# Weight products in runs of eight k, one block of compression products, a 128-row compressed branch, and two more banks for the first output projection

## The chip, the cores and the metric

The kernel runs on one core of a Trainium2 chip. The metric is the device time of one execution in microseconds (us), as the median of several runs. The trace comes from one profiled execution. Engines: PE is TensorE (matrix products; PEld its weight loads), DVE is VectorE, ACT is ScalarE, POOL is GpSimd, SP is the queue that starts the DMA transfers.

## The reference, cut to what matters

A decoder of two layers over 256 tokens of width 1024, all in float32. Layer 0: one input projection feeds forgetting attention (8 heads) and retention (8 heads); their concatenated outputs are gated with SiLU and go through an output projection. Layer 1 is sparse attention with 16 query heads in 4 key groups and three branches: compressed, selected and window, whose outputs are added with gates.

```
def odd_layer(x, norm_g, w_in, b_gate, pe_k, pe_v, wk1, wk2, wv1, wv2, w_out):
    h = rms_norm(x, norm_g)
    u = h @ w_in                       # q, kc, vc, ks, vs, kw, vw, gate, z
    ...
    o = nsa_attention(...)
    return x + (o * jax.nn.silu(z)) @ w_out

def compress_blocks(a, idx, pe, w1, w2):
    ab = a[:, idx] + pe[None, None, :, None, :]       # 15 blocks of 32 tokens
    ab = ab.transpose(0, 1, 3, 2, 4).reshape(B, nc, NSA_KV_GROUPS, l * HEAD_DIM)
    return jax.nn.silu(ab @ w1) @ w2                  # w1: 2048 x 256, w2: 256 x 64

    # inside nsa_attention, per block of queries
    p_cmp = masked_softmax(s_cmp, ...)                # over 15 compressed keys
    o_cmp = jnp.einsum('bghqc,bcgd->bqghd', p_cmp, v_cmp)
    return g[..., 0:1] * o_cmp + g[..., 1:2] * o_slc + g[..., 2:3] * o_win
```

## The kernel before, in words

**Weight products and the feed.** Activations lie transposed: features on the partitions, 256 tokens in the columns. The weights come in 38 chunks of up to 280 columns by 1024 rows. A chunk is loaded by SP into `st`, and split in four quarters into a high half `wh` (fp32r, ScalarE, L95) and a low half `wl` (bf16, VectorE, L102). The activation is held in three forms: high `h`, low `l` (both fp32r) and `b` (bf16). One output tile of 128 columns is a *unit*: 24 products, for each of eight k (blocks of 128 rows) one of `h` and one of `l` with `wh`, and one of `b` with `wl`. `mtile` (L206) and `vtile` (L214) make units, and `runs` (L178) gives the order of their 24 products: `runs(4, 4)` takes `h`, `l` of four k, then `b` of the same four, and that once more. A unit is cut into eight steps of three products, and all steps of the kernel stand in one list, `feed`. `feed.run(n)` issues the next n steps.

**What sets the order.** Everything else (norms, attention, compression) is written by hand between calls of `feed.run`, with the numbers of steps in tuples at the top of the file. PE executes in the order of the code; the scheduler of the framework orders the other engines by it. PSUM, the memory of the products' results, has eight banks: pool `p` two, `s` three, `t` two (transposes), `o` one.

**Output projection of layer 0** (`out_chunks`, L385): eight units `o0_0` to `o0_7`, the first four and the last two k of them interleaved; their ends `o0_done` add the residual, make x1 (`x1h`, `x1l`) and feed the norm. Tiles 0, 1 and 4 to 7 take banks of `p`, 2 and 3 of `s`.

**Compression** (from L702): after the keys of the compressed branch, `build` fills `ab` with the windows. Then 32 fp32 products `ph` (L711), for 8 pairs of rows, two sides and keys or values, add up in the bank of pool `o`; `HW` says how many feed steps stand ahead of them and between the pairs. SiLU of it gives `hid`, which PE transposes (`pth`); two small products give the compressed keys (split into KH and KL) and values `zc`, split into `zch` and `zcl` of 64 rows.

**The loop over t** (L848): for t = 0 to 7 each turn computes, for two heads, scores (`nsa_s`), reductions on VectorE (L774), exponentials on ScalarE (`p`, L786), scaling on GpSimd (L108), the softmax of the compressed scores (`nsa_cmp`: `nsc`, `pc`), transposes back (`nsa_t`, `nsa_c`), and the products with the values (`nsa_o`, L832). In `nsa_o` the compressed branch is two products, `zch` and `zcl` with `ac`, where rows 0 to 31 of `ac` are the transposed probabilities rounded to fp32r and rows 32 to 63 what the rounding left. Between these parts each turn issues 16 feed steps. The loop's part for t − 1 stands inside turn t. Behind the loop the rest of the output projection of layer 1 and the final norm follow.

Of the kernel before, what the change touches and what calls it, by code (L numbers as in the profile page):

```python
# [10 lines left out]
F32 = mybir.dt.float32  # L11
F32R = mybir.dt.float32r
# [25 lines left out]
RR = (2, 0, 9)  # L38
NR = (5, 2, 1, 4, 2, 2)
FS = (2, 1)  # L40
HW = (54, 1, 1, 1, 1, 2, 2, 1, 1)
N8 = (5, 4, 4)
N7 = (4, 3, 2, 3, 0, 6)
HID = (7, 8, 1)
# [9 lines left out]
def trunk_kernel(ctx: ExitStack, tc: tile.TileContext, a: dict):  # L54
# [148 lines left out]
            return step  # L203
        return make

    def mtile(col, xs, kind, name, done, seq=runs(4, 4)):  # L206
# [7 lines left out]
    def vtile(tt, x, kind, name, done, seq=runs(4, 4)):  # L214

        def one(c, p, w, k, start, stop):
            wt, n = c["w"][w == "b"], c["n"]
            T.matmul(p[:, :n], dict(h=x.h, l=x.l, b=x.b)[w][:, k, tt * P:tt * P + P], wt[:, k, :n], start=start, stop=stop)  # L218
        return products(kind, name, lambda c, p: done(p[:, :c["n"]]), seq, one)
# [183 lines left out]
    out_chunks(a["w0o"], lambda: y0, o0_done, "o0_", 4, 7)  # L403


    ab = cp.tile([P, 2, 16, 4, 16], F32, tag="vt_ab", name="ab")
# [57 lines left out]
    def v1_done(c, tt):  # L464
        def done(p):
# [4 lines left out]
            if tt == 1:  # L470
# [2 lines left out]
                V.tensor_scalar(g0, g0, C("rowm"), None, op0=OP.mult)  # L473
        return done

    feed.chunk(a["w1c"][0], 256, [mtile(0, x1, "s", "kc0", c00_done, runs(4, 3, 1)), mtile(1, x1, "s", "kc1", c_done(0, 1), runs(4, 3, 1))],
               [(u, k) for u in range(2) for k in range(7)] + [(0, 7), (1, 7)])
    feed.chunk(a["w1c"][1], 256, [mtile(u, x1, "p", f"vc{u}", c_done(1, u)) for u in range(2)])
    feed.chunk(a["w1c"][2], 256, [mtile(u, x1, "s", f"ks{u}", ks_done(0, u)) for u in range(2)])
# [38 lines left out]
            scale(E["xg"][m], x2[:, m], x2[:, m], gv[:, 16 + m:17 + m])  # L518
        return done

    out_chunks(a["w1o"], lambda: y1, o1_done, "o1_", 5, 6)


    nc.sync.dma_start(gv, a["gv"])
# [210 lines left out]
    zch = cp.tile([64, 2, P], F32R, name="zch")  # L735
    zcl = cp.tile([64, 2, P], F32R, name="zcl")
    for u in range(2):
        pz = bank("t", f"pz{u}")
        for hh in range(2):
            T.matmul(pz[:32, :P], hidT[:, hh, 64 + 32 * u:96 + 32 * u], w2v[:, hh], start=(hh == 0), stop=(hh == 1))  # L740
        zc = wk.tile([32, P], F32, tag="kc", name=f"zc{u}")
        V.tensor_tensor(zc, pz[:32, :P], C("zm")[:32], op=OP.mult)
        for r in range(0, 64, 32):
            V.tensor_copy(zch[r:r + 32, u], zc)
            V.tensor_tensor(zcl[r:r + 32, u], zc, zch[0:32, u].bitcast(F32), op=OP.subtract)
    feed.run(24 - sum(HID) + HID[2])

    y1 = Split("y1", "y")
# [74 lines left out]
    def nsa_c(t):  # L823
        ptC = bank("t", f"ptC_{t}")
        for qt in range(2):
            T.transpose(ptC[:32, qt * P:qt * P + P], PC[t][:, qt].rearrange("p j c -> p (j c)"), ident)
        AC[t] = wk.tile([64, 256], F32R, tag="ac", name=f"ac_{t}")
        copy(E["ac"], AC[t][0:32], ptC[:32, :256])
        V.tensor_tensor(AC[t][32:64], ptC[:32, :256], AC[t][0:32].bitcast(F32), op=OP.subtract)
# [176 lines left out]
```

## Time and profile before

| | |
|---|---|
| median of three runs | 314.49 us (314.44 to 314.97) |
| the profiled execution | 314.97 us |
| its span in the trace | 313.2 us |
| mean granted TensorE clock | 0.988 |
| PE busy | 298.5 us (95%) |
| VectorE busy | 224.5 us (72%) |
| ScalarE busy | 202.5 us (65%) |
| GpSimd busy | 125.6 us (40%) |

The span is the stretch from the first to the last recorded instruction; 1.8 us of the profiled execution lie outside it. An engine's busy time is the union of its instructions' intervals; matrix products overlap in the pipeline, so the start of the next one tells the pace better than the length of one.

### The profile page before, as it was taken

To read this page: it belongs to the slowest core of one execution; us is meant where nothing else is said; L and a number is where in the kernel's file an instruction comes from. 1 tells how busy PE (TensorE), PEld (TensorE's weight loads), DVE (VectorE), ACT (ScalarE), POOL (GpSimd) and SP (SyncE) were. 2 spreads that over 40 slices of the span, in tenths; PEclk is the share of its full clock that TensorE was granted. 3 is DMA by queue.
4 is the path that set the end of the run, shared out by engine and by line. 5 is a ranking of instruction groups with operands and counts; after the bars stand their busy time and mean duration, and the time that the engine had idled before them with its cause. 6 is when DMAs were issued, how large, how long until landed. Compare 5 with 4: busy or idle time off the path is not lost.

```text
span 313.2 us, 6773 instructions
## 1 busy us (share of the span) xinstructions
PE 298.5 (95%) x2478; PEld 261.7 (84%) x2478; DVE 224.5 (72%) x670; ACT 202.5 (65%) x547; POOL 125.6 (40%) x202
## 2 busy tenths in 40 slices
PE   6989999999999999999999999999999999999990
PEld 4879988888988888998996588998898899888970
DVE  2998964665556656289999869787888788882423
ACT  3849555666645555377735476888898898881461
POOL 1430011541522133364300001478778877972242
PEclk9799999999999999999999999999999999999997
DMA  6986798564443333306974433452331233000003
GB/s 170 381 315 238 273 419 335 180 221 143 155 176 134 136 136 136 134 2 214 377 295 150 142 137 125 137 167 104 134 136 28 111 134 136 1 2 0 3 0 134
DMA packets 10978, 49.72 MB, mean 159 GB/s; under 512 B 1601, under 2 KB 2881, under 8 KB 6465
## 3 DMA queue, kind: packets, MB, share of 16 engines
q1 hardware_dynamic: 10656, 49.03, 43.1%
q8 instruction: 19, 0.31, 0.4%
q10 hardware_dynamic: 288, 0.26, 0.3%
q14 instruction: 15, 0.11, 0.1%
HBM read 48.24 MB, written 1.05 MB: 157 GB/s over the span
## 4 chain that ended last, share of the span: by engine, by line
PE 57%; DVE 17%; ACT 17%; issue 3%; POOL 2%; DMA 2%; DVEq 0%; SPq 0%; ACTq 0%; POOLq 0%
PE pp_o L211 10%; ACT p L786 9%; PE pp_q L211 8%; PE pp_k L211 7%; PE pp_z L211 7%; DVE wl L102 6%; PE pp_v L218 5%; ACT wh L95 3%; PE ph L711 3%; PE pp_kw L211 2%; ACT q L95 2%; PE pp_kc L211 2%; PE pp_vc L211 2%; PE pp_ks L211 2%; DMA xT<-in_xT_dram 2%
## 5 line engine op out<-in xcount | busy, mean ns | idle before, releaser
L102 DVE TENSOR_TENSOR wl<-st,wh 128x512 bf16<-128x512 f32 (+2 forms) x152 | 107.6, 737 | 5.9 <-ACT wh L95 5.4
L95 ACT ACTIVATE wh<-st 128x512 fp32r<-128x512 f32 (+2 forms) x151 | 87.5, 621 | 33.5 <-PE pp_o L211 8.0
L108 POOL TENSOR_SCALAR p<-p,st 128x128 f32<-128x128 f32 (+1 forms) x80 | 44.7, 576 | 48.1 <-DVE st L595 31.2
L211 PEld LDWEIGHTS <-wl 128*128 128x128 bf16 x512 | 40.1, 98 | 10.9 <-issue 2.1
L786 ACT ACTIVATE p<-ns,st 128x128 f32<-128x128 f32 (+1 forms) x64 | 28.4, 444 | 5.1 <-DVE st L774 5.0
L102 POOL TENSOR_TENSOR q<-q,q 64x256 fp32r<-64x256 f32 x16 | 12.8, 800 | 42.7 <-ACT q L95 41.5
L218 PE MATMUL pp_v<-wh,x0h 128*128 128x256 f32 (+1 forms) x64 | 19.8, 335 | 2.3 <-ACT wh L95 2.3
L774 DVE CUSTOM_DVE_ANT_0 ns<-s,cst 128x128 f32<-128x128 f32 (+1 forms) x64 | 20.1, 350 | 0.0
L211 PE MATMUL pp_o<-y0h,wh 128*128 128x256 f32 x64 | 17.7, 308 | 0.7 <-DVE xT L380 0.7
L211 PE MATMUL pp_z<-x0h,wh 128*128 128x256 f32 x64 | 18.1, 309 | 0.0
L211 PE MATMUL pp_q<-x0h,wh 128*128 128x256 f32 x64 | 17.7, 309 | 0.0
L211 PE MATMUL pp_q<-x1h,wh 128*128 128x256 f32 x64 | 17.5, 302 | 0.0
L211 PE MATMUL pp_k<-x0h,wh 128*128 128x256 f32 x64 | 17.2, 302 | 0.0
L218 PE MATMUL pp_v<-wh,x0l 128*128 128x256 f32 (+1 forms) x64 | 17.0, 291 | 0.0
L211 PE MATMUL pp_o<-y1h,wh 128*128 128x256 f32 x64 | 16.9, 302 | 0.0
L211 PE MATMUL pp_o<-y1l,wh 128*128 128x256 f32 x64 | 16.8, 288 | 0.0
L211 PE MATMUL pp_z<-x0l,wh 128*128 128x256 f32 x64 | 16.6, 286 | 0.0
L211 PE MATMUL pp_z<-x1h,wh 128*128 128x256 f32 x64 | 16.6, 292 | 0.0
L211 PE MATMUL pp_q<-x1l,wh 128*128 128x256 f32 x64 | 16.1, 280 | 0.0
L211 PE MATMUL pp_o<-y0l,wh 128*128 128x256 f32 x64 | 16.0, 280 | 0.0
L211 PE MATMUL pp_q<-x0l,wh 128*128 128x256 f32 x64 | 16.0, 280 | 0.0
L211 PE MATMUL pp_k<-x0l,wh 128*128 128x256 f32 x64 | 15.8, 280 | 0.0
(322 smaller groups left out, 901.1 us busy)
## 6 DMA issues: line engine op xcount, KB each, us to landing
st<-in_w0c_dram SPq DMA_DIRECT2D x13, 1024.0 KB, 5.0
st<-in_w1c_dram SPq DMA_DIRECT2D x12, 1024.0 KB, 4.9
st<-in_w0o_dram SPq DMA_DIRECT2D x4, 1024.0 KB, 4.9
st<-in_w1o_dram SPq DMA_DIRECT2D x4, 1024.0 KB, 4.8
st<-in_w1v_dram SPq DMA_DIRECT2D x2, 1120.0 KB, 8.0
st<-in_w0c_dram SPq DMA_DIRECT2D x4, 512.0 KB, 7.5
w<-in_wkv_dram SPq DMA_DIRECT2D x4, 512.0 KB, 7.6
w<-in_wkv_dram SPq DMA_DIRECT2D x2, 1024.0 KB, 8.1
```

The lines of the kernel that those rows point to most:

```text
L95: A.activation(o, x, AF.Copy)
L102: (V if e == "V" else G).tensor_tensor(o, x, y, op=op)
L108: (V if e == "V" else G).tensor_scalar(o, x, c, 1.0, op0=OP.mult, op1=OP.mult)
L211: T.matmul(p[:, :S], wt[:, k, col * P:col * P + P], dict(h=x.h, l=x.l, b=x.b)[w][:, k], start=start, stop=stop)
L218: T.matmul(p[:, :n], dict(h=x.h, l=x.l, b=x.b)[w][:, k, tt * P:tt * P + P], wt[:, k, :n], start=start, stop=stop)
L711: T.matmul(ph[64 * kv:64 * kv + 64, :256], ab[:, kv, 2 * qr + j].rearrange("p g c -> p (g c)"), w1[2 * qr + j][:, kv], start=(qr == 0 and ...
L774: V.tensor_tensor_reduce(out=out, in0=pp[:, lo:lo + n], in1=C(tab, lo, lo + n), scale=-slope, scalar=3e38, op0=OP.add, op1=OP.min, accum_o ...
L786: A.activation(p[:, d:d + n], ns[:, d:d + n], AF.Exp, scale=-1.0, bias=st[:, qt, br, 0:1], accum_out=st[:, qt, br, 1:2])
```

## The change

Four things are changed. (1) `runs(8)` takes the place of `runs(4, 4)` in the units: `h`, `l` of all eight k, and then `b` of all eight; the interleaved ones of the output projections go from three stretches to two in the same way, and so do two units of the compressed keys. (2) `HW` puts the 32 `ph` products into one block, after 57 feed steps, with seven behind it. (3) The compressed branch is one product over 128 rows: `zc2` holds value, rounding rest, value, rounding rest in four blocks of 32 rows; GpSimd repeats the probabilities four times (`pc3`, one instruction for each half of the queries) instead of scaling `pc` in place; the transposes give 128 rows, and VectorE's subtraction fills rows 64 to 127 of `ac` with what the rounding left. (4) `out_chunks` takes the banks of its eight tiles as a string: for layer 0 tiles 6 and 7 go to pool `t`; for layer 1 the banks stay as they were.

```
--- before.py
+++ after.py
@@ -38,7 +38,7 @@
 RR = (2, 0, 9)
 NR = (5, 2, 1, 4, 2, 2)
 FS = (2, 1)
-HW = (54, 1, 1, 1, 1, 2, 2, 1, 1)
+HW = (57, 0, 0, 0, 0, 0, 0, 0, 7)
 N8 = (5, 4, 4)
 N7 = (4, 3, 2, 3, 0, 6)
 HID = (7, 8, 1)
@@ -203,7 +203,7 @@
             return step
         return make
 
-    def mtile(col, xs, kind, name, done, seq=runs(4, 4)):
+    def mtile(col, xs, kind, name, done, seq=runs(8)):
 
         def one(c, p, w, k, start, stop):
             x = xs() if callable(xs) else xs
@@ -211,7 +211,7 @@
             T.matmul(p[:, :S], wt[:, k, col * P:col * P + P], dict(h=x.h, l=x.l, b=x.b)[w][:, k], start=start, stop=stop)
         return products(kind, name, lambda c, p: done(p[:, :S]), seq, one)
 
-    def vtile(tt, x, kind, name, done, seq=runs(4, 4)):
+    def vtile(tt, x, kind, name, done, seq=runs(8)):
 
         def one(c, p, w, k, start, stop):
             wt, n = c["w"][w == "b"], c["n"]
@@ -382,12 +382,12 @@
             n1.add(m, xT[:, m])
         return done
 
-    def out_chunks(w, y, done, nm, wide, early):
+    def out_chunks(w, y, done, nm, wide, early, kinds):
 
         units = []
         for m in range(8):
-            units.append(mtile(m % 2, y, "p" if m < 2 or m >= wide else "s", f"{nm}{m}", done(m),
-                               runs(*((4, early - 4, 8 - early) if m < wide else (4, 4)))))
+            units.append(mtile(m % 2, y, kinds[m], f"{nm}{m}", done(m),
+                               runs(*((early, 8 - early) if m < wide else (8,)))))
         start = len(feed.steps)
         for c in range(4):
             feed.chunk(w[c], 256, units[2 * c:2 * c + 2])
@@ -400,7 +400,7 @@
         for c in range(4):
             feed.chunks[-4 + c]["start"] = start + min(i for i, (m, k) in enumerate(order) if m // 2 == c)
 
-    out_chunks(a["w0o"], lambda: y0, o0_done, "o0_", 4, 7)
+    out_chunks(a["w0o"], lambda: y0, o0_done, "o0_", 4, 7, "ppsspptt")
 
 
     ab = cp.tile([P, 2, 16, 4, 16], F32, tag="vt_ab", name="ab")
@@ -473,7 +473,7 @@
                 V.tensor_scalar(g0, g0, C("rowm"), None, op0=OP.mult)
         return done
 
-    feed.chunk(a["w1c"][0], 256, [mtile(0, x1, "s", "kc0", c00_done, runs(4, 3, 1)), mtile(1, x1, "s", "kc1", c_done(0, 1), runs(4, 3, 1))],
+    feed.chunk(a["w1c"][0], 256, [mtile(0, x1, "s", "kc0", c00_done, runs(7, 1)), mtile(1, x1, "s", "kc1", c_done(0, 1), runs(7, 1))],
                [(u, k) for u in range(2) for k in range(7)] + [(0, 7), (1, 7)])
     feed.chunk(a["w1c"][1], 256, [mtile(u, x1, "p", f"vc{u}", c_done(1, u)) for u in range(2)])
     feed.chunk(a["w1c"][2], 256, [mtile(u, x1, "s", f"ks{u}", ks_done(0, u)) for u in range(2)])
@@ -518,7 +518,7 @@
             scale(E["xg"][m], x2[:, m], x2[:, m], gv[:, 16 + m:17 + m])
         return done
 
-    out_chunks(a["w1o"], lambda: y1, o1_done, "o1_", 5, 6)
+    out_chunks(a["w1o"], lambda: y1, o1_done, "o1_", 5, 6, "ppsssppp")
 
 
     nc.sync.dma_start(gv, a["gv"])
@@ -732,17 +732,16 @@
     V.tensor_copy(kcf, pk[:, 0:32].rearrange("p (u c) -> p u c", u=2))
     for u in range(2):
         split_keys(kcf[:, u], u, 256, 16, 0)
-    zch = cp.tile([64, 2, P], F32R, name="zch")
-    zcl = cp.tile([64, 2, P], F32R, name="zcl")
+    zc2 = cp.tile([P, 2, P], F32R, name="zc2")
     for u in range(2):
         pz = bank("t", f"pz{u}")
         for hh in range(2):
             T.matmul(pz[:32, :P], hidT[:, hh, 64 + 32 * u:96 + 32 * u], w2v[:, hh], start=(hh == 0), stop=(hh == 1))
         zc = wk.tile([32, P], F32, tag="kc", name=f"zc{u}")
         V.tensor_tensor(zc, pz[:32, :P], C("zm")[:32], op=OP.mult)
-        for r in range(0, 64, 32):
-            V.tensor_copy(zch[r:r + 32, u], zc)
-            V.tensor_tensor(zcl[r:r + 32, u], zc, zch[0:32, u].bitcast(F32), op=OP.subtract)
+        for r in range(0, P, 64):
+            V.tensor_copy(zc2[r:r + 32, u], zc)
+            V.tensor_tensor(zc2[r + 32:r + 64, u], zc, zc2[0:32, u].bitcast(F32), op=OP.subtract)
     feed.run(24 - sum(HID) + HID[2])
 
     y1 = Split("y1", "y")
@@ -802,8 +801,11 @@
             V.tensor_reduce(out=sc, in_=pc, op=OP.add, axis=mybir.AxisListType.X)
             V.reciprocal(sc, sc)
             V.tensor_tensor(sc, sc, gate[:, :, 6 * t:6 * t + 6:3], op=OP.mult)
-            binary(E["cs"][1], pc, pc, sc.unsqueeze(3).to_broadcast([P, 2, 2, 16]), OP.mult)
-            PC[t] = pc
+            pc3 = wk.tile([P, 2, 4, 2, 16], F32, tag="pc3", name=f"pc3_{t}")
+            for qt in range(2):
+                binary(E["cs"][1], pc3[:, qt], pc[:, qt].unsqueeze(1).to_broadcast([P, 4, 2, 16]),
+                       sc[:, qt].unsqueeze(1).unsqueeze(3).to_broadcast([P, 4, 2, 16]), OP.mult)
+            PC[t] = pc3
 
     def nsa_t(t, j):
         p = PX[t, j]
@@ -823,16 +825,15 @@
     def nsa_c(t):
         ptC = bank("t", f"ptC_{t}")
         for qt in range(2):
-            T.transpose(ptC[:32, qt * P:qt * P + P], PC[t][:, qt].rearrange("p j c -> p (j c)"), ident)
-        AC[t] = wk.tile([64, 256], F32R, tag="ac", name=f"ac_{t}")
-        copy(E["ac"], AC[t][0:32], ptC[:32, :256])
-        V.tensor_tensor(AC[t][32:64], ptC[:32, :256], AC[t][0:32].bitcast(F32), op=OP.subtract)
+            T.transpose(ptC[:, qt * P:qt * P + P], PC[t][:, qt].rearrange("p r j c -> p (r j c)"), ident)
+        AC[t] = wk.tile([P, 256], F32R, tag="ac", name=f"ac_{t}")
+        copy(E["ac"], AC[t], ptC[:, :256])
+        V.tensor_tensor(AC[t][64:], ptC[64:, :256], AC[t][64:].bitcast(F32), op=OP.subtract)
 
     def nsa_o(t):
         u = t // 4
         po = bank("o", f"po1_{t}")
-        T.matmul(po[:, :S], zch[:, u], AC[t], start=True, stop=False)
-        T.matmul(po[:, :S], zcl[:, u], AC[t], start=False, stop=False)
+        T.matmul(po[:, :S], zc2[:, u], AC[t], start=True, stop=False)
         for br in range(2):
             for kt in range(2):
                 for j in range(2):
```

On PE, in the stretch of the second window key (`pp_kw`, two units), before: the `ph` products stand in groups of four between the steps of the feed, the first groups between products with the high half, then between those with the low half.

```order
L211 MATMUL pp_kw_2228<-x1h,wh_2116 128x256
L211 MATMUL pp_kw_2228<-x1l,wh_2116 128x256
L711 MATMUL ph<-w_0_1705,ab 64x256 x4
L211 MATMUL pp_kw_2228<-x1h,wh_2116 128x256
L211 MATMUL pp_kw_2228<-x1l,wh_2116 128x256
L211 LDWEIGHTS wl_2117
L211 MATMUL pp_kw_2228<-x1b,wl_2117 128x256
L711 MATMUL ph<-w_1_1707,ab 64x256 x4
L211 LDWEIGHTS wl_2117
L211 MATMUL pp_kw_2228<-x1b,wl_2117 128x256
```

After: all of them stand in a row (the names in it are the loaded blocks of w1), in the second `pp_kw` unit.

```order
L211 MATMUL pp_kw_2270<-x1l,wh_2116 128x256
L211 MATMUL pp_kw_2270<-x1h,wh_2116 128x256
L711 MATMUL ph<-w_0_1705,ab 64x256 x4
L711 MATMUL ph<-w_1_1707,ab 64x256 x4
L711 MATMUL ph<-w_2_1709,ab 64x256 x4
L711 MATMUL ph<-w_3_1980,ab 64x256 x8
L711 MATMUL ph<-w_4_1982,ab 64x256 x8
L711 MATMUL ph<-w_5_1984,ab 64x256 x4
L211 MATMUL pp_kw_2270<-x1l,wh_2116 128x256
```

The block begins in the middle of a unit's products with the high half and goes back to them.

On PE, in the loop's turn t = 3 (the values of head pair 2), before: the two products of the compressed branch stand at the head of `nsa_o`, behind the first transpose of `nsa_t`.

```order
L813 MATMUL ptA_3282<-cst,p_3137 128x128
L834 MATMUL po_2_3249<-ac_3240,zch 128x256
L835 MATMUL po_2_3249<-ac_3240,zcl 128x256
L842 MATMUL po_2_3249<-a_20_3098,vs 64x256
L842 MATMUL po_2_3249<-a_21_3177,vs 64x256
```

After, one product of 128 rows (line numbers move by one or two):

```order
L815 MATMUL ptA_3284<-cst,p_3138 128x128
L836 MATMUL po_2_3252<-ac_3243,zc_2447 128x256
L843 MATMUL po_2_3252<-a_20_3099,vs 64x256
L843 MATMUL po_2_3252<-a_21_3180,vs 64x256
L843 MATMUL po_2_3252<-a_20_3104,vs 64x128
```

One product has gone; what follows is as before.

On GpSimd, one turn of the loop, before: `pc` is scaled in place by one instruction of 64 columns, behind the gate and the split of y1.

```order
L102 TENSOR_TENSOR q_4_3189<-q_4_3187,q_4_3189 64x256 x2
L102 TENSOR_TENSOR nsc_3134<-nsc_3134,mxc_3135 128x64
L108 TENSOR_SCALAR p_3204<-p_3204,st_3205 128x128 x2
L108 TENSOR_SCALAR p_3204<-p_3204,st_3205 128x256 x2
L102 TENSOR_TENSOR sz(1, 3)_3277<-sz(1, 3)_3277,z(1, 3)_3275 128x256
L102 TENSOR_TENSOR y1l<-y_2_3260,y1h 128x256
L99 TENSOR_SCALAR y1b<-y1h 128x256
L102 TENSOR_TENSOR pc_3352<-pc_3352,sc_3356 128x64
L108 TENSOR_SCALAR p_3326<-p_3326,st_3327 128x128 x2
```

After, two of 128 columns, one ahead of the split of y1 and one behind the gate:

```order
L102 TENSOR_TENSOR q_4_3192<-q_4_3190,q_4_3192 64x256 x2
L102 TENSOR_TENSOR nsc_3135<-nsc_3135,mxc_3136 128x64
L108 TENSOR_SCALAR p_3207<-p_3207,st_3208 128x128 x2
L108 TENSOR_SCALAR p_3207<-p_3207,st_3208 128x256 x2
L102 TENSOR_TENSOR pc_3_3362<-pc_3354,sc_3358 128x128
L102 TENSOR_TENSOR y1l<-y_2_3262,y1h 128x256
L99 TENSOR_SCALAR y1b<-y1h 128x256
L102 TENSOR_TENSOR sz(1, 3)_3279<-sz(1, 3)_3279,z(1, 3)_3277 128x256
L102 TENSOR_TENSOR pc_3_3362<-pc_3354,sc_3358 128x128
L108 TENSOR_SCALAR p_3328<-p_3328,st_3329 128x128 x2
```

The gate `sz` moves behind the split of y1, and the first `pc3` stands ahead of both.

## Rows read from the trace of the kernel before

**Rows 1.** Page, busy time, share of the span and instructions of each engine

```profile
PE 298.5 (95%) x2478; PEld 261.7 (84%) x2478; DVE 224.5 (72%) x670; ACT 202.5 (65%) x547; POOL 125.6 (40%) x202
```

**Rows 2.** Busy windows: window, us, engines' busy us (instructions), granted clock, DMA share, GB/s

```profile
154.00:167.50 13.50, 13.50 (x117) 12.80 (x116) 13.21 (x26) 4.88 (x12) 0.00 (x0) 1.00 0.71 274
226.60:237.30 10.70, 10.70 (x96) 9.59 (x94) 9.02 (x43) 9.20 (x30) 8.40 (x16) 1.00 0.28 100
280.00:304.00 24.00, 24.00 (x211) 21.59 (x207) 9.51 (x23) 10.09 (x25) 9.53 (x15) 1.00 0.01 1
```

**Rows 3.** Chain of waits, 226 to 238: start, us, piece of the chain

```profile
226.48 0.71 POOL nsc L102
...
237.13 0.70 POOL nsc L102
```

**Rows 4.** Waits, 215 to 280: engine, line, releaser; us in total, times, longest

```profile
PEld po L834 <- DVE ac L829: 1.3, 6, 0.4
```

**Rows 5.** Timeline of PE: start, us, line, operation, out<-in, shape, count

```profile
104.58 0.36 PE L211 MATMUL pp_z<-x0h,wh 128*128 128x256 f32 x1
104.78 0.28 PE L211 MATMUL pp_z<-x0l,wh 128*128 128x256 f32 x1
...
105.62 0.61 PE L211 MATMUL pp_z<-x0b,wl 128*128 128x256 bf16 x4
105.99 0.36 PE L211 MATMUL pp_z<-x0h,wh 128*128 128x256 f32 x1
```

**Rows 6.** Timeline of PE, first `ph` group, and the tile's products (ns min/median/max)

```profile
167.44 0.28 PE L211 MATMUL pp_kw<-x1l,wh 128*128 128x256 f32 x1
167.65 1.08 PE L711 MATMUL ph<-w,ab 128*64 128x256 f32 x8
168.66 0.39 PE L211 MATMUL pp_kw<-x1h,wh 128*128 128x256 f32 x1
168.89 0.27 PE L211 MATMUL pp_kw<-x1l,wh 128*128 128x256 f32 x1
...
L711 PE MATMUL ph<-w,ab x64: 379/379/430, 167.6 to 179.9; 128*64 128x256 f32 x64
```

**Rows 7.** Timelines of PE and VectorE, output projection of layer 0

```profile
144.47 0.39 PE L211 MATMUL pp_o<-y0h,wh 128*128 128x256 f32 x1 [0.75 <-DVE xT L380]
...
151.98 0.61 DVE L119 SCALAR_TENSOR_TENSOR x1l<-xT,gv,x1h 128x256 fp32r<-128x256 f32 x1
```

**Rows 8.** Timeline of VectorE; in brackets the idle time before and its releaser

```profile
178.07 0.69 DVE L102 TENSOR_TENSOR wl<-st,wh 128x512 bf16<-128x512 f32 x1
180.74 0.29 DVE L454 TENSOR_TENSOR kf<-pp_kw,R_n 128x128 f32<-128x128 f32 x1 [1.97 <-PE pp_kw L211]
```

**Rows 9.** Chain of waits, 184 to 196.5

```profile
184.93 0.35 DVE hid L718
...
195.95 0.39 PE s L763
```

**Rows 10.** Timeline of PE, the last head's compressed products but one

```profile
279.13 0.38 PE L834 MATMUL po<-ac,zch 64*128 64x256 f32 x1
279.35 0.28 PE L835 MATMUL po<-ac,zcl 64*128 64x256 f32 x1
```

**Rows 11.** Timelines of VectorE and GpSimd, one turn of the loop

```profile
226.35 0.68 DVE L102 TENSOR_TENSOR wl<-st,wh 128x512 bf16<-128x512 f32 x1
...
226.48 0.70 POOL L102 TENSOR_TENSOR nsc<-nsc,mxc 128x64 f32<-128x64 f32 x1
...
229.75 0.74 POOL L102 TENSOR_TENSOR sz(1, 2)_3088<-sz(1, 2)_3088,z(1, 2)_3086 128x256 f32<-128x256 f32 x1 [0.53 <-ACT sz(1, 2)_3088 L264]
...
231.53 0.30 POOL L102 TENSOR_TENSOR pc<-pc,sc 128x64 f32<-128x64 f32 x1
233.36 2.07 POOL L108 TENSOR_SCALAR p<-p,st 128x128 f32<-128x128 f32 x4 [1.53 <-ACT a L95]
```

More of the change, by code (lines that the diff above doesn't have):

```diff
@@ L40 @@
 FS = (2, 1)
-HW = (54, 1, 1, 1, 1, 2, 2, 1, 1)
+HW = (57, 0, 0, 0, 0, 0, 0, 0, 7)
 N8 = (5, 4, 4)
@@ L204, in products, with mtile @@
         return make
-    def mtile(col, xs, kind, name, done, seq=runs(4, 4)):
+    def mtile(col, xs, kind, name, done, seq=runs(8)):
         def one(c, p, w, k, start, stop):
@@ L212, in mtile, with vtile @@
         return products(kind, name, lambda c, p: done(p[:, :S]), seq, one)
-    def vtile(tt, x, kind, name, done, seq=runs(4, 4)):
+    def vtile(tt, x, kind, name, done, seq=runs(8)):
         def one(c, p, w, k, start, stop):
@@ L383, in o0_done, with out_chunks @@
         return done
-    def out_chunks(w, y, done, nm, wide, early):
+    def out_chunks(w, y, done, nm, wide, early, kinds):
         units = []
         for m in range(8):
-            units.append(mtile(m % 2, y, "p" if m < 2 or m >= wide else "s", f"{nm}{m}", done(m),
-                               runs(*((4, early - 4, 8 - early) if m < wide else (4, 4)))))
+            units.append(mtile(m % 2, y, kinds[m], f"{nm}{m}", done(m),
+                               runs(*((early, 8 - early) if m < wide else (8,)))))
         start = len(feed.steps)
@@ L401, in out_chunks @@
             feed.chunks[-4 + c]["start"] = start + min(i for i, (m, k) in enumerate(order) if m // 2 == c)
-    out_chunks(a["w0o"], lambda: y0, o0_done, "o0_", 4, 7)
+    out_chunks(a["w0o"], lambda: y0, o0_done, "o0_", 4, 7, "ppsspptt")
     ab = cp.tile([P, 2, 16, 4, 16], F32, tag="vt_ab", name="ab")
@@ L474, in v1_done @@
         return done
-    feed.chunk(a["w1c"][0], 256, [mtile(0, x1, "s", "kc0", c00_done, runs(4, 3, 1)), mtile(1, x1, "s", "kc1", c_done(0, 1), runs(4, 3, 1))],
+    feed.chunk(a["w1c"][0], 256, [mtile(0, x1, "s", "kc0", c00_done, runs(7, 1)), mtile(1, x1, "s", "kc1", c_done(0, 1), runs(7, 1))],
                [(u, k) for u in range(2) for k in range(7)] + [(0, 7), (1, 7)])
@@ L519, in o1_done @@
         return done
-    out_chunks(a["w1o"], lambda: y1, o1_done, "o1_", 5, 6)
+    out_chunks(a["w1o"], lambda: y1, o1_done, "o1_", 5, 6, "ppsssppp")
     nc.sync.dma_start(gv, a["gv"])
@@ L734, in trunk_kernel @@
         split_keys(kcf[:, u], u, 256, 16, 0)
-    zch = cp.tile([64, 2, P], F32R, name="zch")
-    zcl = cp.tile([64, 2, P], F32R, name="zcl")
+    zc2 = cp.tile([P, 2, P], F32R, name="zc2")
     for u in range(2):
@@ L742, in trunk_kernel @@
         V.tensor_tensor(zc, pz[:32, :P], C("zm")[:32], op=OP.mult)
-        for r in range(0, 64, 32):
-            V.tensor_copy(zch[r:r + 32, u], zc)
-            V.tensor_tensor(zcl[r:r + 32, u], zc, zch[0:32, u].bitcast(F32), op=OP.subtract)
+        for r in range(0, P, 64):
+            V.tensor_copy(zc2[r:r + 32, u], zc)
+            V.tensor_tensor(zc2[r + 32:r + 64, u], zc, zc2[0:32, u].bitcast(F32), op=OP.subtract)
     feed.run(24 - sum(HID) + HID[2])
@@ L804, in nsa_cmp @@
             V.tensor_tensor(sc, sc, gate[:, :, 6 * t:6 * t + 6:3], op=OP.mult)
-            binary(E["cs"][1], pc, pc, sc.unsqueeze(3).to_broadcast([P, 2, 2, 16]), OP.mult)
-            PC[t] = pc
+            pc3 = wk.tile([P, 2, 4, 2, 16], F32, tag="pc3", name=f"pc3_{t}")
+            for qt in range(2):
+                binary(E["cs"][1], pc3[:, qt], pc[:, qt].unsqueeze(1).to_broadcast([P, 4, 2, 16]),
+                       sc[:, qt].unsqueeze(1).unsqueeze(3).to_broadcast([P, 4, 2, 16]), OP.mult)
+            PC[t] = pc3
     def nsa_t(t, j):
@@ L825, in nsa_c @@
         for qt in range(2):
[L826 to L829, printed above, removed]
+            T.transpose(ptC[:, qt * P:qt * P + P], PC[t][:, qt].rearrange("p r j c -> p (r j c)"), ident)
+        AC[t] = wk.tile([P, 256], F32R, tag="ac", name=f"ac_{t}")
+        copy(E["ac"], AC[t], ptC[:, :256])
+        V.tensor_tensor(AC[t][64:], ptC[64:, :256], AC[t][64:].bitcast(F32), op=OP.subtract)
     def nsa_o(t):
@@ L833, in nsa_o @@
         po = bank("o", f"po1_{t}")
-        T.matmul(po[:, :S], zch[:, u], AC[t], start=True, stop=False)
-        T.matmul(po[:, :S], zcl[:, u], AC[t], start=False, stop=False)
+        T.matmul(po[:, :S], zc2[:, u], AC[t], start=True, stop=False)
         for br in range(2):
```

## The prediction

> **What bounds the kernel now.** I read the page's busy times first, then the busy windows of three stretches, then the chain of waits, then the timelines of single engines. PE is busy for 298.5 us of a span of 313.2, VectorE for 224.5 [rows 1]. So PE looks like the bound everywhere. The windows take that apart [rows 2]: from 154.0 to 167.5 PE has no gap at all, but VectorE is busy for 13.21 of the 13.50 too; from 280 to 304 PE alone is full; and in one turn of the loop over the second layer's heads (226.6 to 237.3) PE is full by the counter while VectorE, ScalarE and GpSimd have 9.02, 9.20 and 8.40 of 10.70. The granted clock is full (1.00) in all three, so nothing below hangs on it.
>
> A busy counter does not say who waits. In the loop the chain goes from one POOL `nsc` to the next through VectorE, ScalarE and GpSimd, with no PE piece in it, and the turn is 237.13 − 226.48 = 10.65 us [rows 3]. PE waits for them there: the weight load of the compressed branch's product waits for VectorE's `ac` in six turns, 1.3 us in all, though PE shows no gap because the products before it are still draining [rows 4]. So a PE saving counts in the tail, counts before the loop as far as VectorE has room, and counts for nothing inside the loop.
>
> The profiled execution took 314.97 us (span 313.2, so 1.8 lie around it); the median of the three runs is 314.49. I make the sum as differences on the trace and take them off the median.
>
> **Runs of eight k.** A unit (two per chunk, 38 chunks) goes from two stretches of fp32r and two of bf16 products to one of each; 74 of the 76 lose one pair of switches. What a switch costs: twelve products of `pp_z`, eight fp32r and four bf16, take 105.99 − 104.58 = 1.41 us [rows 5]. Eight steps of .12 and four of .11 are 1.40. The step behind a bf16 product is longer (104.58 to 104.78 is .20), but the last bf16 step is shorter by as much, because the records overlap. So a pair of switches costs about .01 and at most .02; nothing excludes 0. That is 74 × .01 = .7 us of PE time over the kernel, 0 to 1.5. Some 34 units lie before the first output projection, .34 us; there four retention blocks and one value block now come back to fp32r products where they came back to bf16, and the first step behind an fp32 block is .23 instead of .12 [rows 6], 5 × .11 = .55 at worst. I take 0 for that part (−.7 to +.4). Some 32 units lie where others decide. Only the eight of the tail count: −.1. The other side of it: the low half of the weights (`wl`) is wanted later, which no stage can lose by.
>
> **Two more banks for o0.** PE waited .75 us at 144.47 for VectorE's `xT`, which frees the bank of an earlier output tile [rows 7]. With tiles 6 and 7 in the two transpose banks that wait can go. But what PE needs next is x1 of all eight tiles: VectorE's last `x1l` is at 151.98 [rows 7], its list of work up to there is the same as before, and from there to 167.5 it is the dense one [rows 2]. PE would only arrive earlier at the same wait. Value 0, bounds 0 to −.75.
>
> **The compression products in one block.** Before, eight groups of four fp32 products (eight records each) stand between `pp_kw` products. One group: 167.65 to the next product's start at 168.66 is 1.01; the entry is .21 where a step is .12 (167.44 to 167.65), and the step after it is .23 where .12 would do [rows 6]. Eight groups are 8 × (1.01 + .09) plus .11 for the five or so that are left into fp32r, about 9.4 us. Inside a group the records start in pairs. The last starts 1.08 − .38 = .70 after the first, and I read the .05 by which the longest record exceeds the usual one (430 to 379 ns) as the first pair's extra [rows 6]: (.70 − .05) / 3 = .217 a pair. One block of 64 records is 32 pairs: 31 × .217 + .05 + .31 (from the last start to the next product, 168.66 − 168.35) + .20 for entry and exit = 7.3. PE saves 2.1 us. The trace shows no such block longer than eight records, so I bound the step by .217 below and by .27 above (the first pair's step, .217 + .05, held throughout); at .27 the block is 8.9 and the saving .5.
>
> Can the end use it? All inputs are there: the block begins three feed steps later than the first group did, and `ab` was ready for that one. What waits for PE is VectorE: it ends a `wl` at 178.07 + .69 and then stands idle for 1.97 until `pp_kw` releases `kf` at 180.74 [rows 8]. So PE's 2.1 can be passed on up to 1.97, then VectorE's own list is late. Behind `kf` VectorE goes on without PE deciding: `hid` at 184.93, and on to the first scores at 195.95 [rows 9]. One more `wh` now stands ahead of ScalarE's small key copies there, but it is free to start as much earlier. Value −1.9; bounds −.5 (the slow pair step) to −2.1.
>
> **The compressed branch as one product.** In each of eight heads one product `po<-ac,zcl` goes: 279.13 to 279.35, .22 us [rows 10], 1.76 in all. Six lie in the loop, where PE waits for `ac` itself; a product less behind a wait shortens nothing that the chain goes through: 0 (bounds 0 to −1.3). Two (`po_6`, `po_7`) lie where PE is full to the end: −.44. What is added: the transposes give 128 rows, the same count of columns; ScalarE's and VectorE's other work keeps its size in columns. GpSimd gets two products `pc3` of 128 columns for one of 64. The trace has no GpSimd product of that form: between .30 for the 64 columns of `pc` and .74 for the 256 of `sz` I put .45 [rows 11], so +.60 a turn (bounds +.3 to +1.2). Behind `pc` GpSimd idled 1.53 before `p` at 233.36, which it got from ScalarE's `a` [rows 11], so .60 is covered; 1.2 would be as well.
>
> The price of `pc` hangs on its neighbour, though: `nsc`, also 64 columns, takes .70 where a `wl` of VectorE runs from 226.35 to 227.03, and `pc` .30 where none runs [rows 11]. The Trainium skill says more of this ("SBUF — State Buffer", section "Who interferes with whom"): a VectorE instruction with two inputs in SBUF and a GpSimd instruction share a port, whoever has it holds it for the whole instruction, and the other is stopped. The trace agrees as far as .70 against .30 goes; by that rule the doubled `pc3` would cost VectorE its own duration wherever it gets in ahead of a `wl`. That is the second rival below.
>
> **Sum.** −1.9 (block) −.44 (tail products) −.1 (tail switches) + 0 for the rest = −2.45. 314.49 − 2.45 = 312.04, so 312.0 us.
>
> **Rivals.**
> A: *PE is the bound everywhere, and every PE saving reaches the end.* For it: 95% busy, no gap in the loop's window. Against it: the wait row of `ac` and the chain. It gives −2.1 −1.76 −.7 (switches), with the .75 of o0 −5.3: 309.2 to 310.0. The Trainium skill ("Perfetto Trace Analysis", section "Identifying the Most-Contended Engine") would have the engine with the most busy time be the one to shorten; by that sentence it would be this rival. The trace speaks against it in the loop.
> B: *GpSimd's `pc3` holds up VectorE in the loop; slower.* In the new order the first `pc3` is released just as the third `wl` of a turn begins, and that `wl` stands right ahead of the score reductions that the chain goes through. If GpSimd goes first, VectorE loses .45 in each of seven turns, 3.2 us: 312.0 + 3.2 = 315.2. It decides from .35 a turn on (2.45 / 7). For it: the .70 of `nsc`. Against it: in before it was GpSimd's instruction that was stretched, not the `wl` (.68, like all others). Half of it gives 313.6.
> C: *A long fp32 block does not keep the short step.* At .27 it saves .5 instead of 1.9: 313.4. For it: nothing longer than eight records was seen. Against: within eight the step does not grow.
> D: *The saving before the loop is met by another wait* (VectorE's dense list ahead of 167.5, or the small key copies behind ScalarE's extra `wh`, .55), and the tail's .54 alone is left: 313.9, no change that could be told.
>
> **How the numbers follow.** The forecast as worked out, 311.4 to 312.7: .55. A: .15. C or half of B, 312.7 to 313.8: .15. D and other ways to nothing: .07. B in full: .08. The measurement can tell .2% (.63 us), so faster means under 313.86: .55 + .15 + .15 = .85; same .07; slower .08. The range leaves out most of A's lower half, B in full and part of D: 309.8 to 313.9. The forecast's own range is 311.4 to 312.7.
>
> **What would show it.** VectorE's idle before `kf` falls from 1.97 to near 0 and the block of 64 records takes 7.3 us: right; 8.9: C. The first scores come 1.9 earlier, at about 194.0. The turn of the loop stays 10.65; 10.4 or less would be A, 11.0 B, with `wl` or the reductions longer next to `pc3`. The tail from the last loop turn is shorter by .5. PE's wait at 144.47 goes and the first product of x1 starts no earlier. If the loop's turn moves by more than .1 in either direction, or if the first scores come less than 1 us earlier, the forecast is wrong in its reasons.

## The result and the profile after

The changed kernel takes 310.89 us (median of 4 runs, 310.71 to 311.04) against 314.47 for the one before: a ratio of 0.9884, 95% interval 0.9872 to 0.9896, so 3.6 us faster. The forecast was 312.0, its own range 311.4 to 312.7, the full range 309.8 to 313.9. The gain is 1.1 us larger than forecast, and the runs below show in which term.

The profiled execution took 311.04 us, its span is 309.2. The first weight product starts at 7.85 in it and at 8.13 in before; from profile to profile this start moves by up to .7 us, whatever the kernel, so milestones below are compared from that product on or as differences.

The page's busy line of after (as [rows 1]):

```profile
PE 294.5 (95%) x2470; PEld 264.0 (85%) x2470; DVE 224.6 (73%) x670; ACT 202.1 (65%) x547; POOL 130.6 (42%) x210
```

**The block.** PE's timeline of after, the `ph` products (as [rows 6]):

```profile
168.28 7.13 PE L711 MATMUL ph<-w,ab 128*64 128x256 f32 x64
175.34 0.39 PE L211 MATMUL pp_kw<-x1l,wh 128*128 128x256 f32 x1
```

64 records from 168.28 to the next product at 175.34 are 7.06; with .09 for the entry and .11 for the exit 7.25, where 7.3 was worked out. The short pair step holds over the whole block. VectorE's timeline behind it (as [rows 8]) and the first scores on the chain of waits (as [rows 9]):

```profile
176.54 1.90 DVE L102 TENSOR_TENSOR wl<-st,wh 128x512 bf16<-128x512 f32 x3
178.35 0.28 DVE L454 TENSOR_TENSOR kf<-pp_kw,R_n 128x128 f32<-128x128 f32 x1
```

```profile
193.66 0.39 PE s L762
```

The idle time of 1.97 ahead of `kf` is gone: the row has no bracket. The first scores come at 193.66 − 7.85 = 185.81 after the first weight product, 187.82 in before: 2.0 earlier.

**The two banks.** PE's timeline of after, the first products with x1 (as [rows 7]):

```profile
147.71 0.38 PE L211 MATMUL pp_kc<-x1h,wh 128*128 128x256 f32 x1 [0.35 <-ACT x1h L106]
148.90 0.38 PE L211 MATMUL pp_kc<-x1l,wh 128*128 128x256 f32 x1 [0.81 <-DVE x1l L119]
```

The wait of .75 for `xT` is gone, and two waits, .35 and .81, stand in its place a few us on.

**The loop.** GpSimd's timeline of after, the start of two turns (as [rows 3]), and the chain's shares in 224 to 235:

```profile
224.10 0.80 POOL L102 TENSOR_TENSOR nsc<-nsc,mxc 128x64 f32<-128x64 f32 x1
...
234.59 0.80 POOL L102 TENSOR_TENSOR nsc<-nsc,mxc 128x64 f32<-128x64 f32 x1
```

```profile
by line: PE pp_z L211 25.3%; PE pp_q L211 25.2%; PE po L843 18.1%; PE ptA L815 9.3%; PE s L763 6.8%; PE s L762 6.7%; PE ptB L820 4.0%; PE po L836 2.8%; PE ptC L828 2.0%
```

The turn is 10.49 instead of 10.64, .15 that the forecast did not have, and the chain, which had no PE in it before, is now PE alone. The chain now says "PE". The experiments below show that PE does not set this turn.

**The tail.** PE's timeline of after, the compressed product of the last head but one (as [rows 10]):

```profile
275.64 0.28 PE L211 MATMUL pp_o<-y1h,wh 128*128 128x256 f32 x1
275.75 0.31 PE L836 MATMUL po<-ac,zc 128*128 128x256 f32 x1
275.99 0.44 PE L843 MATMUL po<-a,vs 128*64 128x256 f32 x2
```

From the last loop `nsc` (269.04 before, 266.05 after) to the final norm's product on PE (303.67 and 299.72) it is 34.63 before and 33.67 after: .96 less, .54 were forecast. So the sum is 2.0 + .75 (five turns) + .96, less .05 between the first scores and the loop: 3.66, against 3.58 by the medians.

### The profile page after: what moved, and what is told of

It reads as the page before. It is cut to its first block, busy times and chain, and to the rows that moved or that the text cites. A ratio compares the mean times of both kernels' runs of the same rounds, so it can differ in the third digit from the quotient of the medians.

```text
span 309.2 us, 6770 instructions
## 1 busy us (share of the span) xinstructions
PE 294.5 (95%) x2470; PEld 264.0 (85%) x2470; DVE 224.6 (73%) x670; ACT 202.1 (65%) x547; POOL 130.6 (42%) x210
## 4 chain that ended last, share of the span: by engine, by line
PE 68%; DVE 18%; ACT 5%; DMA 4%; issue 2%; SPq 1%; POOL 0%; DVEq 0%; ACTq 0%; POOLq 0%
PE pp_z L211 13%; PE pp_q L211 12%; PE pp_o L211 11%; PE pp_k L211 7%; DVE wl L102 7%; PE pp_v L218 5%; PE po L843 4%; DMA st<-in_w0c_dram 3%; DVE ab L102 3%; DVE KL L102 2%; PE ptA L815 2%; DMA xT<-in_xT_dram 2%; ACT p L785 2%; ACT wh L95 2%; PE s L762 2%
## 5 line engine op out<-in xcount | busy, mean ns | idle before, releaser
L108 POOL TENSOR_SCALAR p<-p,st 128x128 f32<-128x128 f32 (+1 forms) x80 | 43.1, 555 | 39.6 <-DVE st L595 32.0
L211 PEld LDWEIGHTS <-wl 128*128 128x128 bf16 x512 | 44.3, 98 | 7.8 <-issue 0.7
L211 PE MATMUL pp_z<-x0h,wh 128*128 128x256 f32 x64 | 16.8, 298 | 0.0
L211 PE MATMUL pp_o<-y0h,wh 128*128 128x256 f32 x64 | 16.7, 297 | 0.0
L218 PEld LDWEIGHTS pp_v<-wh,x0h 128*128 128x128 f32 x64 | 13.6, 212 | 3.3 <-ACT wh L95 2.9
L211 PE MATMUL pp_k<-x0h,wh 128*128 128x256 f32 x64 | 16.3, 292 | 0.0
L211 PE MATMUL pp_q<-x1h,wh 128*128 128x256 f32 x64 | 16.2, 292 | 0.0
L211 PE MATMUL pp_o<-y1h,wh 128*128 128x256 f32 x64 | 16.0, 293 | 0.0
L211 PE MATMUL pp_z<-x1l,wh 128*128 128x256 f32 x64 | 15.9, 282 | 0.0
```

The source lines that it names most:

```text
L108: (V if e == "V" else G).tensor_scalar(o, x, c, 1.0, op0=OP.mult, op1=OP.mult)
```

## The experiments

**One part at a time.** Four kernels, each before with one of the four edits alone: e1_runs8 has only

```
-    def mtile(col, xs, kind, name, done, seq=runs(4, 4)):
+    def mtile(col, xs, kind, name, done, seq=runs(8)):
...                      (vtile, out_chunks and kc in the same way)
```

e2_block only the line of `HW`, e3_zc only `zc2`, `pc3` and the 128 rows of `ac`, e4_banks only the tiles' bank strings.

> Before, with the runs of eight k alone. Theory (the loop's turn holds a PE stretch, so PE savings count there in part; the runs themselves save only a switch of about .01 a unit): the turn of the loop stays within .04 of 10.64, the tail is .1 to .4 shorter, the whole 0.2 to 0.7 us faster (313.8 to 314.3). Rival (it is the runs of eight that made the loop's turn .15 shorter): turn 10.5, the whole 1.2 us faster or more (313.2 or less).

> Before, with the compression products in one block alone. Theory: the block takes about 7 us, PE comes 2.1 to 2.3 earlier out of it, VectorE's idle before kf goes, the first scores come 1.9 earlier, and the loop and tail are as before: 312.5 us (-1.9). Rival (a part of that comes from the other edits): 313.0 to 313.6.

> Before, with the compressed branch as one product of 128 rows alone (pc3 on GpSimd with it). Theory (PE's own stretch from one value product to the next scores lies in the loop's cycle): the turn falls from 10.64 to about 10.48, and with two products of .22 in the tail the whole is 1.3 us faster (313.2). Rival, as I forecast (the turn is set by VectorE, ScalarE and GpSimd alone): the turn stays 10.64, the whole is .45 faster (314.0). Rival of a slower GpSimd: the turn is over 10.64.

> Before, with the two more banks for the output tiles alone. Theory: PE's wait of .75 for xT goes and the first pp_kc product starts about .8 earlier, but waits of about the same size for x1h and x1l follow in pp_kc, and pp_vc starts within .2 of before: no change, 314.3 to 314.6. Rival (the wait removed reaches the end): 313.7.

Measured, against 314.46 in the same runs: e1 314.30 (ratio 0.9994, 0.9986 to 1.0003), e2 312.48 (0.9937, 0.9924 to 0.9951), e3 312.83 (0.9949, 0.9937 to 0.9962), e4 314.54 (1.0001, 0.9992 to 1.0010). The four differences, −.16, −1.98, −1.63 and +.08, add up to −3.69, within the noise the whole change (−3.58 by the medians): the parts don't help or hinder each other in the total. Runs of eight and banks are no change that can be told; the block is worth what was forecast; the compressed product is worth 1.63 where .44 was forecast. In e3 the turn is 10.48, in e1, e2 and e4 10.63 to 10.64.

Two expectations were off in the tail. e1's was to be .1 to .4 shorter and is not (34.62 against 34.63): .11 is won behind the last compressed product, and as much is lost ahead of it, where PE waits longer for `ac`. e3 is .4 faster than its theory said, and its tail, 33.74, is .89 shorter where .44 was put.

In e4 the wait that replaces the other is a single one of .81 for x1l, and `pp_vc` starts 146.01 after the first product, in before 146.02.

**Why the loop's turn fell.** e3 takes one product from PE in each turn (worth .12 there, as e5 shows below), but the order of the instructions shows a second thing: with that product gone the scheduler orders the other engines another way. In the loop VectorE's copy of `a` and its small product `sc` (128x4, scale times gate) now stand ahead of the third `wl`, and GpSimd's `sz` stands behind the split of y1. Timelines of VectorE and GpSimd in before around `sc` (GpSimd's row is in [rows 11]), and VectorE's in after, with GpSimd's of after behind them:

```profile
230.13 0.38 DVE L804 TENSOR_TENSOR sc<-sc,gate 128x4 f32<-128x4 f32 x1
```

```profile
227.24 0.15 DVE L803 TENSOR_TENSOR sc<-sc,gate 128x4 f32<-128x4 f32 x1
227.31 0.68 DVE L102 TENSOR_TENSOR wl<-st,wh 128x512 bf16<-128x512 f32 x1
```

```profile
227.54 0.71 POOL L102 TENSOR_TENSOR pc<-pc,sc 128x128 f32<-128x128 f32 x1 [0.60 <-ACT a L95]
228.22 0.73 POOL L102 TENSOR_TENSOR y1l<-y,y1h 128x256 fp32r<-128x256 f32 x1
228.92 0.40 POOL L99 TENSOR_SCALAR y1b<-y1h 128x256 bf16<-128x256 f32 x1
229.29 0.74 POOL L102 TENSOR_TENSOR sz(1, 2)_3089<-sz(1, 2)_3089,z(1, 2)_3087 128x256 f32<-128x256 f32 x1
229.99 0.40 POOL L102 TENSOR_TENSOR pc<-pc,sc 128x128 f32<-128x128 f32 x1
```

In before, `sz` runs from 229.75 to 230.49, and `sc`, started at 230.13, ends at 230.51: it takes .38 for four columns. In after nothing of GpSimd runs beside it and it takes .15. VectorE's score reductions, and with them ScalarE's exponentials, stand right behind. So there were two candidates, PE's missing product and VectorE's .23, and the next runs part them.

e5_nozcl is before with one line less:

```
-        T.matmul(po[:, :S], zcl[:, u], AC[t], start=False, stop=False)
```

> Before, with the product of zcl left out (the rounding rest of the compressed values is not added) and nothing else: no 128 rows, no pc3. If the loss of that one product is what made the loop's turn shorter in the run of part 3, the turn is 10.48 and the whole 312.8 us, as there. If the 128-row form or the new GpSimd products did it, the turn stays 10.64 and the whole is 314.0 (two products of .22 in the tail).

e7_order is after with one line more, which costs PE next to nothing and brings the old order back:

```
         T.matmul(po[:, :S], zc2[:, u], AC[t], start=True, stop=False)
+        T.matmul(po[:32, :32], zc2[:, u, :32], AC[t][:, :32], start=False, stop=False)
```

> After, with one tiny product (32 x 32) more behind the compressed one in each turn (it adds a doubled value to a corner of the result). It costs PE some hundredths of a us, but the scheduler now orders VectorE, ScalarE and GpSimd in the loop as in the kernel before (sz ahead of the copy of a, the third wl ahead). If PE's time is what counts, the turn is 10.49 to 10.55 and the whole 311.0 to 311.4 us; if the new order of the other engines made the turn shorter, it goes back to 10.64 and the whole is 311.9 or more.

e8_less_pe is after without one product of the scores (`KL` for the third tile of the second head; the product ahead of it then ends the sum):

```
-            T.matmul(o[:, :n], q[:, j, qs], KL[:, g, cs], start=False, stop=True)
+            if not (j == 1 and o is sC):
+                T.matmul(o[:, :n], q[:, j, qs], KL[:, g, cs], start=False, stop=True)
```

> After, with one more PE product of .12 left out in each turn (the low half of the keys for the last score tile of the second head); VectorE's order is that of after. If PE sets the turn now, it falls from 10.49 to about 10.36 and the whole is .9 us faster (310.0). If the other engines set it, the turn stays 10.49 and the whole is .1 to .25 faster (310.7).

Measured: e5 313.32 (0.9965, 0.9952 to 0.9977), e7 311.91 (0.9920, 0.9906 to 0.9933), e8 310.66 (0.9881, 0.9867 to 0.9894). e7's turn goes to 10.72, longer than before's, with `sc` at .37 again; e8's stays at 10.49 though PE has .12 less to do: by these two the other engines set the turn of after, and the reading of e3 as "PE's stretch" falls. In e8 the chain of the same stretch has no PE in it, and PE's weight load waits longer for `ac` (in four turns; columns as in [rows 4]):

```profile
PEld po L838 <- DVE ac L833: 1.2, 4, 0.3
```

e5 is the odd one: its time lies between the two that were expected (312.8 and 314.0). Its first two turns are 10.40 and 10.38, the last three 10.50 to 10.52, with the chain on PE. That asked for the opposite test, `sc` out of VectorE's way with PE's work left alone:

```
-            V.tensor_tensor(sc, sc, gate[:, :, 6 * t:6 * t + 6:3], op=OP.mult)
+            G.tensor_tensor(sc, sc, gate[:, :, 6 * t:6 * t + 6:3], op=OP.mult)
```

in before (e9), in the kernel of e7 (e10) and in after (e11).

> Before, with the small product of the compressed branch's scale and its gate (sc, 128x4) moved from VectorE to GpSimd; the orders of PE and ScalarE stay, VectorE's only loses that row. Theory (in before this 128x4 product takes .38 instead of .15 in each loop turn because GpSimd's sz holds the port that both need, and the turn waits for it): the turn falls by .2 to .25, to 10.40 to 10.45, or to 10.50 where PE becomes the limit, and the whole is 313.1 to 313.7 us. Rival (the .23 is hidden): 10.64 and 314.4.

> The kernel of the order run (after, with the tiny product that brings the old order of the other engines back, turn 10.72), and the same small product on GpSimd. Theory: the turn falls to about 10.50 and the whole to 310.6 us, the order no longer matters once VectorE has nothing there for the port to stop. Rival (the order acts in another way): 10.72 and 311.9.

> After, with the same small product on GpSimd. In after it already runs unhindered (.15). Theory: VectorE is spared .07 to .15 a turn on the chain, the turn is 10.38 to 10.49, the whole 310.2 to 310.9 us. Rival (GpSimd's added instruction delays pc3 or the next turn): over 311.2.

Measured: e9 314.27 (0.9993, 0.9984 to 1.0001), e10 310.39 (0.9878, 0.9863 to 0.9893), e11 310.83 (0.9880, 0.9867 to 0.9894). e9 misses: its first turn is 10.38, and from then on it is 10.63, with the chain on PE alone. PE itself has the long turn from the first one on (`po<-ac` starts at 214.20, 224.84, 235.48 and 246.11); only GpSimd's `nsc` got ahead once. e10 is as expected or better: 10.72 falls to 10.41. GpSimd's timeline of e9:

```profile
215.40 0.72 POOL L102 TENSOR_TENSOR nsc<-nsc,mxc 128x64 f32<-128x64 f32 x1
225.78 0.70 POOL L102 TENSOR_TENSOR nsc<-nsc,mxc 128x64 f32<-128x64 f32 x1
236.41 0.70 POOL L102 TENSOR_TENSOR nsc<-nsc,mxc 128x64 f32<-128x64 f32 x1
```

Put together (mean turn from the second `nsc` of the loop's steady part to the sixth):

| kernel | PE's work in a turn | `sc` on VectorE | turn, us |
|---|---|---|---|
| before | as it was | .38 | 10.64 |
| e1 | two switches less | .38 | 10.63 |
| e9 | as it was | moved away | 10.63 |
| e5 | one product less | .15 | 10.38, then 10.51 |
| e3 | one product less | .15 | 10.48 |
| after | both less | .15 | 10.49 |
| e8 | both and .12 less | .15 | 10.49 |
| e7 | both less | .37 | 10.72 |
| e10, e11 | both less | moved away | 10.41 |

Which limit a kernel stands at can be read from one weight load, that of the compressed product `po<-ac`, and from the end of VectorE's `ac` that it needs. Timelines of VectorE, of the weight loads and of PE's transposition ahead of them, one turn each of before, e9, after and e11:

```profile
235.44 0.41 DVE L829 TENSOR_TENSOR ac<-ptC,ac 32x256 fp32r<-32x256 f32 x1
235.90 0.18 PEld L834 LDWEIGHTS po<-ac,zch 64*128 64x128 f32 x1 [0.17 <-DVE ac L829]
```

```profile
234.74 0.41 DVE L829 TENSOR_TENSOR ac<-ptC,ac 32x256 fp32r<-32x256 f32 x1
235.28 0.27 PE L813 MATMUL ptA<-cst,p 128*128 128x128 f32 x1
235.48 0.18 PEld L834 LDWEIGHTS po<-ac,zch 64*128 64x128 f32 x1 [0.17 <-issue]
```

```profile
232.92 0.43 DVE L831 TENSOR_TENSOR ac<-ptC,ac 64x256 fp32r<-64x256 f32 x1
233.40 0.19 PEld L836 LDWEIGHTS po<-ac,zc 128*128 128x128 f32 x1 [0.17 <-DVE ac L831]
```

```profile
232.11 0.43 DVE L831 TENSOR_TENSOR ac<-ptC,ac 64x256 fp32r<-64x256 f32 x1
232.48 0.27 PE L815 MATMUL ptA<-cst,p 128*128 128x128 f32 x1
232.60 0.19 PEld L836 LDWEIGHTS po<-ac,zc 128*128 128x128 f32 x1
```

In before, after and e11 the load starts .05 to .06 behind the end of `ac`; in e9 `ac` has ended .33 ahead of it. The other turns and kernels divide in the same way: .05 to .06 in e1, e3, e7, e8 and e10, .18 to .31 in e5. So e9 and e5 stand at PE's limit. All others of the table stand at that of the other engines, those too whose chain names PE alone (after, e3, e10, e11).

Before stood at two limits at once. Taking PE's work alone away (a little in e1, all that the change takes in e7) or the other engines' delay alone (e9) leaves the turn at 10.63 or more; both together (e3, e5, after) give 10.5. PE's own limit was 10.63 (e9), is 10.51 without the product (e5), and 10.41 or less in the changed kernel (e10, e11). The others' limit was 10.64, is 10.49 in the new order (e8), and 10.41 with `sc` moved as well (e10, e11).

Of the .22 or more by which PE's limit fell, .12 are the product (e9 to e5). Another .08 or more come from the 128-row form itself, which no expectation had: the step from the transposition `ptA` to the compressed product is .20 with the 64 rows of `zch` even where `ac` is long ready (e9, e5), and at most .12 with the 128 rows of `zc` (e10, e11; .16 to .19 in e3, with runs of four, though it waits for `ac` there). The runs of eight give the rest, .02 to .04 a turn.

**The block's cover.** e6_quarter_ph sums only the first and the last of the eight pairs of rows:

```
-        for j in range(2):
+        for j in range(0 if qr in (0, 7) else 2, 2):
```

> After, with 24 of the 32 compression products left out (only the first and last pair of rows are summed): PE sheds 24 x .217 = 5.2 us in the block. Theory (behind the block VectorE's own list is the limit, PE's saving of after already filled its idle time): the first scores come at most .5 earlier, the whole 310.4 to 310.9 us. Rival (PE sets the end there): 305.7.

Measured: 310.53 (0.9886, 0.9865 to 0.9906). The first scores come 185.83 after the first weight product, in after 185.81. PE's timeline of e6 shows where the PE time goes:

```profile
174.52 0.37 PE L218 MATMUL pp_v<-wh,x1h 128*128 128x280 f32 x1 [1.56 <-DVE kf L455]
...
179.07 0.37 PE L218 MATMUL pp_v<-wh,x1h 128*128 128x280 f32 x1 [1.29 <-DVE kf L455]
...
183.02 0.44 PE L722 MATMUL pth<-cst,hid 128*128 128x128 f32 x2 [2.15 <-DVE hid L718]
```

Of these waits after has only a part of the last:

```profile
182.93 0.44 PE L722 MATMUL pth<-cst,hid 128*128 128x128 f32 x2 [0.59 <-DVE hid L718]
```

1.56 + 1.29 + 2.15 − .59 = 4.4: most of the 5.2 that PE sheds is waited away at VectorE within these 9 us, and none of it reaches the first scores. The change took from this place all that could be passed on.

**VectorE's list, then.** e12_ab_pool is e11 with `ab="VVVG"` for `ab="VVVV"`: a quarter of the additions of `ab` on the idle GpSimd.

> As the last, and a quarter of the additions that build ab (4 of 16, 64x240, two inputs in SBUF) moved from VectorE to the idle GpSimd, in the stretch where VectorE is the limit ahead of the block. If both engines can work side by side, VectorE is spared 4 x .58 = 2.3 us and the first scores come 1 to 2 us earlier (309 to 310). If an instruction of GpSimd holds VectorE's two-input instructions for as long as it runs, nothing is won or up to 3 us are lost (310.5 to 313.5); I hold this for likelier.

Measured: 309.91 (0.9859, 0.9846 to 0.9873). The first scores come 185.89 after the first weight product, no earlier than in after: nothing was won where the edit is. Timelines of VectorE and GpSimd in e12:

```profile
155.69 2.52 DVE L102 TENSOR_TENSOR ab<-kc,pe 64x240 f32<-64x240 f32 x3
```

```profile
155.68 1.60 POOL L102 TENSOR_TENSOR ab<-kc,pe 64x240 f32<-64x240 f32 x2 [3.17 <-DVE kc L427]
```

Three additions take VectorE 2.52 while GpSimd does two; in after eight take 4.63, so three would be 1.74. Over the whole stretch VectorE's additions take 8.64 where after has 9.25: of the 2.3 us of work that went to GpSimd, VectorE is spared .6 and waits the rest. That .6 is gone by the next keys, since VectorE's order changed too and two `wl` now stand ahead of their `kf`. The median of e12 is the lowest of all, .9 under e11, but every milestone of the two traces lies within .1 us (loop 10.41, tail 34.4), so I do not claim that .9 for the edit. e10, e11 and e12 lie at or under after in the median; their intervals overlap with its own, so a version that surely beats it was not shown. In e11 two effects nearly cancel: five turns of the loop are .08 shorter each, but the tail is 34.44 where after and e10 have 33.67, because PE waits there for `ac` ahead of the last compressed product but one. PE's timeline of e11:

```profile
275.38 0.39 PE L836 MATMUL po<-ac,zc 128*128 128x256 f32 x1 [0.50 <-DVE ac L831]
```

## Why the prediction was right, and where it was wrong

The direction was right. The time, 310.89, lies under the forecast's own range (311.4 to 312.7) and inside the full one, which reaches down for rival A; that it lies there is owed to no step of its reasoning on the loop.

**The block: right**, in mechanism and size. Worked out: 7.3 us of block, 2.1 saved, 1.97 of it usable, value −1.9. Measured: 7.25, idle time gone, first scores 2.0 earlier, −1.98 alone. e6 shows the limit: more PE time saved there is worth nothing. Rival C falls by the block's 7.25, rival D by the first scores.

**The banks: right.** Value 0, measured +.08 within its interval; the wait is turned into another for VectorE's `x1l`.

**Runs of eight: right**, as far as it can be told. −.1 was put, −.16 measured alone, which cannot be told from 0. The size of the step holds too: PE's turn less the step into the compressed product, where any wait for `ac` lies, is about 10.43 in before and 10.39 in e1, 10.30 in e3 and 10.29 in after. That is .01 to .02 for each of the two units of a turn, where .01 and at most .02 was put. In e1 the .04 came to nothing: PE waited that much longer for `ac`.

**The compressed branch: wrong, and this is the whole error.** The step was "a product less behind a wait shortens nothing that the chain goes through: 0". By the prediction's own sign, a turn that moves by more than .1, its reasons are wrong here (10.49 instead of 10.64). Three things in it failed. First, the wait row of [rows 4], .2 in each turn for `ac`, was read as PE standing still. It is not: in e9, where `ac` ends .33 ahead of the load, the same weight load has the same .2, now put down to "issue" (row of e9, four turns):

```profile
PEld po L834 <- issue: 0.7, 4, 0.2
```

PE had no slack in before, its own limit of 10.63 was as good as reached. Second, the edit's effect on VectorE was seen in the order of instructions only as GpSimd's: the same shift that put `pc3` early also took `sc` out from beside `sz`, .23 a turn on the chain. The prediction had looked at the port only for the harm that `pc3` might do. Third, the sizes: the product was priced at .22, its distance to the next one, but without it the step behind its neighbour grows, and e5 against e9 gives .12; the step into the compressed product, .08 or more shorter with 128 rows, was put at nothing.

**Rival B: no.** `pc3` starts at 227.54, .23 into a `wl` that began at 227.31; the `wl` takes its usual .68, and `pc3` .71 instead of the .40 of the free one at 229.99 (.45 was put). GpSimd came second and paid. The Trainium skill ("SBUF — State Buffer", section "Who interferes with whom") says that issue order decides who blocks. This case shows both directions, `sc` behind `sz` and `pc3` behind `wl`. So the rule the prediction weighed was right, and its sign in this change was the other one: it spoke for the change.

**Rival A: no, but nearer than the forecast in the loop.** PE's saving counted up to the others' limit, and no further. In the tail .96 were measured against .54. The two products are not .44 but .24 (e5 has .12 less between its last two compressed products and .11 behind them). The step into the last but one falls from .38 to .12, since `ac` comes earlier against PE there, and that into the last from .21 to .03. The runs of eight give .11 behind the last one, as in e1. The rest, .15 to .2, I cannot assign.

**Still open.** In all kernels with `pc3` VectorE's `z` starts about .1 later behind the reciprocal ahead of it, which would fit e7's turn of 10.72 instead of 10.64; neither this nor what holds `z` was tried. Nor was what holds `ac` at 10.41 in e10 and e11.

## What to carry to other kernels

A loop can stand at two limits at once: then taking away either alone shows nothing, and the chain of waits can name the wrong one, since it decides by hundredths. Test it from both sides, one run with less work on the named engine and one with its competitor relieved. Before a wait row is called slack, look whether the same gap stands there when the releaser is early, and compare the releaser's end with the start of what it releases. When a scheduler orders the engines, read the whole new order of the engines on the chain, not only the rows of the edit: here a PE product less also moved a small instruction on VectorE, and only both together shortened the turn.

## What the runs showed of the hardware

- A VectorE product of four columns with both inputs in SBUF takes .15 alone and .38 beside a GpSimd product of 256 columns that began before it; a GpSimd product of 128 columns takes .40 alone and .71 beside a VectorE one that began before it.
- 64 fp32 records in a row keep the short pair step: the first of 31 is .266 us, the others are .216 (.217 was worked out from groups of eight).
- From a transposition over 128 rows to an fp32r product over 64 rows PE's step is .20 where nothing is waited for (e9, e5); to one over 128 rows it is .12 or less (e10, e11).
- Four of sixteen two-input additions moved to GpSimd (.7 to 1.1 each there) spare VectorE, which has the same kind to do, .6 of their 2.3 (9.25 to 8.64); the rest it waits.
